# Which engine adds up the weights for a Strassen-like product: trading VectorE adds against DMA sums between two matrix products

## The chip, the cores and the metric

The kernel runs on one core of a Trainium2 chip. The metric is the device time of one execution in microseconds; lower is better. TensorE (PE) does the matrix products, VectorE (DVE) and ScalarE (ACT) prepare operands and empty PSUM, GpSimd (POOL) and SyncE (SP) mostly issue DMAs.

## The reference, cut to what matters

The reference is one layer of a streaming encoder on a (512, 1024) float32 stream: attention in two branches, a gated merge, then an MLP and a gated embedding, each with its RMSNorm. The change touches only the weights of the MLP:

```python
u = rms_norm(h, g_mlp)
h = h + jnp.square(jax.nn.relu(u @ w_ff1)) @ w_ff2      # w_ff1 (1024, 4096), w_ff2 (4096, 1024)
```

All of it is float32, and the tolerance asks for more than one rounded product, so every matrix is split into a rounded part (hi) and a remainder (lo), and each product is made as hi*hi + hi*lo + lo*hi.

## The kernel before, in words

**Seven products instead of eight.** ff1 (u @ w_ff1) and ff2 (... @ w_ff2) are cut into eight groups each of 512 hidden columns. A group's weights are a 2x2 arrangement of quadrants of [128, 1024] float32 (512 KB), named (0,0), (1,0), (0,1), (1,1). A group is made with seven products of sums, Winograd's form of Strassen's scheme, rather than eight plain ones. Products 1, 2 and 3 use a quadrant as it was loaded. The other four use sums that are made in place:

- product 5: (0,0) += (0,1)
- product 6: the same place += (1,1), after product 5's weights have been split
- product 4: the same place += (1,0), after product 6's weights have been split
- product 7: (0,1) += (1,1), after product 5's sum has read (0,1)

**Who makes a sum.** `sum_source` (line 276) makes it, either as `tensor_tensor` on VectorE (line 296) or as an accumulating DMA that GpSimd issues (line 298). Before the change: ff2's (key "s2") products 5 and 7 on VectorE, and ff1's group 1 products 6 and 7 too; all others by DMA. That is 18 VectorE sums and 46 DMAs in the feed-forward part. Eight further DMA sums are for the gates (`wgw`), earlier in the kernel.

**A split** (`emit_split`, lines 301 to 326) makes hi with a ScalarE cast (line 324) and lo with a VectorE subtraction (line 325). The traces name them `u<n>h` and `u<n>l`, n counting all weight units.

**Order.** The feed-forward part runs in four passes (fq = 0..3) of 28 products each. Pass fq has ff1's groups 2fq (letter a) and 2fq + 1 (letter b), and ff2's same groups (A and B):

```python
STEPS = "a1 b1 a2 a5 b5 b2 a6 b6 a7 a3 b7 b3 A1 a4 b4 B1 A2 A5 B5 B2 A6 B6 A3 A7 B7 B3 A4 B4"
```

Unit 53 is a1 of pass 0, and each pass has 28 units: u109 to u136 are pass 2. In it u113 is b5, u116 b6, u117 a7, u126 A5, u127 B5, u130 B6, u131 A3 and u132 A7. A product is 24 matmuls of 256 columns (`win_mm`, line 918, traced as `('f1', g)x`, y or z by its PSUM bank) or 12 of 512 (`s2_mm`, line 1331, `s_0x` and so on). Products 1, 6, 7 and 4 of a group add into the same bank x, and what they held is copied or drained in between: ff1 by `win_out` (lines 929 and 933), ff2 by `h_add` into the residual stream (lines 1073 and 1075) after the odd group.

**What sets the order.** Instructions of TensorE and GpSimd run in the order in which the program traces them. For VectorE, ScalarE and the loads on SP a planner puts them in order at build time by costs and due times of its own, in nearly all of the passes. On the chip every engine runs its list strictly in that order. In step n the main loop (line 1369) first takes out the product before, then splits the weights of step n + 2 (`advance`), offers step n + 3 to `sum_source` (line 388), and then traces product n.

`advance` also offers sums as soon as they may be made: after product 1's split product 5's sum, after 5's split those of 6 and 7, after 6's split that of 4. The condition in line 339 left ff2's 5 and 7 out of this; they came by line 388 (and the planner could still put them earlier on VectorE).

**Places.** Twelve places of 512 KB hold the quadrants; a load may start once the last reader of the quadrant before it has been split.

Of the kernel before, what the change touches and what calls it, by code (L numbers as in the profile page):

```python
# [50 lines left out]
def layer_kernel(ctx: ExitStack, tc: tile.TileContext, x, p, g_mix, w_in, b_forget, swa_sinks,  # L51
# [32 lines left out]
    raws, order, unit_of = [], [], {}  # L84
# [94 lines left out]
    def raws_of(i):  # L179
        r, pn = order[i][1][:2]  # L180
        if isinstance(r, dict):
            return [r[z] for z in {1: ((0, 0),), 2: ((1, 0),), 3: ((1, 1),),
                                   5: ((0, 0), (0, 1)), 6: ((0, 0), (1, 1)),
                                   7: ((0, 1), (1, 1)), 4: ((0, 0), (1, 0))}[pn]]
        if isinstance(r, list):
            return {1: r[:1], 2: r[1:], 3: r[1:]}.get(pn, r)
        return [r]
# [58 lines left out]
    def emit_dma(i):  # L246

        upto = max(first_raw[r] for r in raws_of(i))
        while look["d"] <= upto:
            r_ = used[look["d"]]  # L250
            r = raws[r_]
            if r_ in before and before[r_] >= look["n"]:
                return
            if first_ff <= r_ < last_ff:
                if "place" not in look:
                    return
                r["tile"] = ff_place(place_of[r_], r["shape"])
            elif place_of[r_]:
                if look["wp2"] is None:
                    return  # L260
                r["tile"] = look["wp2"].tile(r["shape"], F32, tag="w2_raw", bufs=2, name=r["name"])
            else:
                r["tile"] = wp.tile(r["shape"], F32, tag="w_raw", bufs=2, name=r["name"])
            for ks, src in r["fns"]:
                nc.sync.dma_start(r["tile"][:, ks], src)
            look["d"] += 1

    def quadrant(i, h, e):


        rs = order[i][1][0]
        return raws[rs[h]]["tile"][:, e] if isinstance(rs, list) else raws[rs[h, e]]["tile"]
# [3 lines left out]
    def sum_source(i):  # L276

        if i in sources or i >= len(order) or not isinstance(order[i][1][0], (list, dict)):  # L280
            return
        emit_dma(i)
        key, (rs, pn, _), _ = order[i]

        first = {5: 1, 6: 5, 4: 6}.get(pn)
        if (first and unit_of[key[:-1] + (first,)] >= look["n"]
                or pn == 7 and unit_of[key[:-1] + (5,)] not in sources
                or any(raws[r]["tile"] is None for r in raws_of(i))):
            return
        if pn in (1, 2, 3):  # L290
            q = quadrant(i, pn in (2, 3), pn == 3)
        else:
            q = quadrant(i, 0, pn == 7)
            other = quadrant(i, *{5: (0, 1), 7: (1, 1), 6: (1, 1), 4: (1, 0)}[pn])
            if key[0] == "s2" and pn in (5, 7) or key in (("f1", 1, 6), ("f1", 1, 7)):
                nc.vector.tensor_tensor(q, q, other, ALU.add)
            else:
                nc.gpsimd.dma_start(q, other, accum_op=ALU.add)  # L298
        sources[i] = q if key[0] == "s2" else q.rearrange("q k (j c) -> q k j c", c=P)

    def emit_split(i):
        _, (r, sl, shape), _ = order[i]
        emit_dma(i)
        if order[i][0] in early:
            hi, lo = early[order[i][0]]
        else:
            hi = wp.tile(shape, F32R, tag="w_hi", bufs=4, name=f"u{i}h")
            lo = wp.tile(shape, F32R, tag="w_lo", bufs=4, name=f"u{i}l")
        sum_source(i)
        src = sources[i] if isinstance(r, (list, dict)) else raws[r]["tile"][sl]  # L310
        if order[i][0][0] == "pg":

            for a in range(2):
                g = g_ple_t[:, 2 * order[i][0][2] + a:2 * order[i][0][2] + a + 1]
                nc.scalar.mul(hi[:, a], src[:, a], g)
                nc.vector.scalar_tensor_tensor(lo[:, a], src[:, a], g, hi[:, a].bitcast(F32),
                                               ALU.mult, ALU.subtract)
            order[i][2] = (hi, lo)
            return
        np_ = N_PIECES if i < 20 else 1  # L320
        for a in range(np_):
            n = shape[1] // np_
            z = slice(a * n, a * n + n)
            nc.scalar.copy(hi[:, z], src[:, z])
            nc.vector.tensor_tensor(lo[:, z], src[:, z], hi[:, z].bitcast(F32), ALU.subtract)  # L325
        order[i][2] = (hi, lo)

    def advance(i):

        while look["n"] < min(len(order), i + 1):  # L330
            n = look["n"]
            emit_split(n)
            look["n"] += 1
            emit_dma(min(len(order) - 1, look["n"] + look["ahead"]))
            if isinstance(order[n][1][0], (list, dict)):

                key = order[n][0]
                for pn in {1: (5,), 5: (6, 7), 6: (4,)}.get(key[-1], ()):
                    if key[0] != "s2" or pn in (6, 4):
                        sum_source(unit_of[key[:-1] + (pn,)])  # L340

    def unit(key):
        i = unit_of[key]
        advance(i + look["split"])
        if i == 0:
            emit_dma(look["dma"])
        return order[i][2]
# [674 lines left out]
    for t in P2_STEPS:  # L1022
        if t[0] == "ops":
            gate_ops(t[1])
            continue
        if t[0] == "fill":
            look["split"] = 2
            fill(t[1])
            look["split"] = 0
            continue  # L1030
        i = unit_of[t]
        if done is not None and done[0] == "g":
            gate_out(win_out(done[:3], done[3], tmp2), done[1])
        advance(i + 3)
        for n in range(look["n"], i + 9):
            sum_source(n)
        if t[0] == "br":
            branches(t[1])
            if t[1] == 5:
                h_sb = hp.tile([P, NT, D], F32, tag="h", bufs=1, name="h_sb")  # L1040
                nc.sync.dma_start(h_sb, x.rearrange("(t q) d -> q t d", q=P))
                gb = hp.tile([P, D], F32, tag="gb", bufs=1, name="g_mlp_bc")
                bcast_row(gb, g_mlp[0])
        else:
            win_mm(t[:3], t[3], [[o] for o in g_op[t[3]]], {})
        done = t
# [191 lines left out]
    for tb in range(NT - 1):  # L1238
        h2(tb, 1, row_group("psm", "mix", mix_t, 1, tb))
        scale2(tb)  # L1240
        if tb == 0:
            advance(unit_of["pp", 1])
        if tb > 0:
            t2_pe(tb - 1)
            t2_top(tb - 1)
# [272 lines left out]
```

## Time and profile before

| | |
|---|---|
| median of 3 runs | 715.89 us (715.85 to 716.19) |
| the profiled execution | 717.25 us, its span 715.3 us |
| busy: PE, DVE, ACT, POOL | 704.4, 532.7, 450.2, 84.8 us |
| granted TensorE clock, mean | 0.997 |
| the four passes | about 352 to 660 us |
| VectorE sums / DMA sums, feed-forward part | 18 / 46 |

The span is the time from the first instruction to the last; an execution takes some 2 us more. Rows of the timelines give the start in us, the duration, engine, line, operation, and in square brackets the idle time of the engine before it and what ended it. Rows of the chain of waits give start, length and what ran. "PEld" is the loading of weights into TensorE, which shows a wait for an operand first. The ends of matmuls are modelled, so a product's length is best taken from start to start.

### The profile page before, as it was taken

To read this page: it belongs to the slowest core of one execution; us is meant where nothing else is said; L and a number is where in the kernel's file an instruction comes from. 1 tells how busy PE (TensorE), PEld (TensorE's weight loads), DVE (VectorE), ACT (ScalarE), POOL (GpSimd) and SP (SyncE) were. 2 spreads that over 40 slices of the span, in tenths; PEclk is the share of its full clock that TensorE was granted. 3 is DMA by queue.
4 is the path that set the end of the run, shared out by engine and by line. 5 is a ranking of instruction groups with operands and counts; after the bars stand their busy time and mean duration, and the time that the engine had idled before them with its cause. 6 is when DMAs were issued, how large, how long until landed. Compare 5 with 4: busy or idle time off the path is not lost.

```text
span 715.3 us, 11466 instructions
## 1 busy us (share of the span) xinstructions
PE 704.4 (98%) x4229; PEld 626.4 (88%) x4229; DVE 532.7 (74%) x908; ACT 450.2 (63%) x839; POOL 84.8 (12%) x124
## 2 busy tenths in 40 slices
PE   8999999999999999999999999999999999999995
PEld 7988888888888998888899889988999789988885
DVE  6557888877696556545789985899579966997565
ACT  6547888779863554344788736874477546875452
POOL 1011211100001200001510102010300021010101
PEclk9999999999999999999999999999999999999998
DMA  9256456670364795450885598739894699079002
GB/s 288 70 164 159 115 125 158 151 196 1 119 206 118 147 320 181 152 172 31 238 188 193 111 288 160 239 86 256 185 253 119 152 243 233 34 148 351 3 22 96
DMA packets 74055, 115.67 MB, mean 162 GB/s; under 512 B 6664, under 2 KB 44560, under 8 KB 74000
## 3 DMA queue, kind: packets, MB, share of 16 engines
q1 hardware_dynamic: 65936, 86.24, 38.0%
q0 software_dynamic: 7776, 28.32, 21.5%
q8 instruction: 33, 0.54, 0.3%
q10 hardware_dynamic: 288, 0.39, 0.2%
q14 instruction: 22, 0.18, 0.1%
HBM read 72.93 MB, written 4.19 MB: 108 GB/s over the span
## 4 chain that ended last, share of the span: by engine, by line
PE 86%; DVE 6%; DMA 4%; issue 2%; ACT 1%; POOL 0%; SPq 0%; POOLq 0%; DVEq 0%; ACTq 0%
PE pf L74 5%; PE pf L76 5%; PE pf L75 5%; PE s_6x L1331 3%; PE s_0x L1331 3%; PE h_sc L760 3%; PE s_2x L1331 2%; PE h_pv L830 2%; PE h_tr L818 2%; PE psm L76 2%; PE psm L74 2%; PE psy L74 2%; PE psy L75 2%; PE psm L75 2%; PE psy L76 2%
## 5 line engine op out<-in xcount | busy, mean ns | idle before, releaser
L298 POOL DMA_DIRECT2D wq<-wq x24 | 21.8, 936 | 166.8 <-DVE u70l L325 25.9
L778 ACT ACTIVATE s<-s,h_nm 128x128 f32<-128x128 f32 (+1 forms) x64 | 32.6, 512 | 5.9 <-DVE h_nm L771 5.1
L71 DVE TENSOR_TENSOR h_ptl<-h_tr,h_pth 128x512 fp32r<-128x512 f32 (+2 forms) x40 | 22.9, 604 | 4.0 <-ACT h_pth L70 3.6
L359 POOL TENSOR_SCALAR n_ms<-acc 128x1 f32<-128x1 f32 x15 | 5.6, 373 | 163.8 <-ACT junk L1083 105.4
L70 ACT CAST h_pth<-h_tr 128x512 fp32r<-128x512 f32 (+2 forms) x40 | 19.4, 523 | 1.8 <-PE h_tr L818 1.4
L70 ACT CAST u<-n_tr 128x512 fp32r<-128x512 f32 (+2 forms) x26 | 12.6, 519 | 11.8 <-PE n_tr L1139 5.6
L474 PE MATMUL va<-wv_h,u 128*128 128x320 f32 x64 | 20.0, 317 | 0.0
L818 PE MATMUL h_tr<-ident,s 128*128 128x128 f32 x136 | 19.6, 277 | 0.2
L474 PE MATMUL vb<-wv_h,u 128*128 128x328 f32 x64 | 19.6, 313 | 0.0
L71 DVE TENSOR_TENSOR u<-n_tr,u 128x512 fp32r<-128x512 f32 (+2 forms) x26 | 15.0, 603 | 5.8 <-ACT u L70 5.7
L298 POOL DMA_DIRECT2D wgw<-wgw x8 | 7.1, 971 | 102.3 <-DVE u25l L325 77.7
L1083 ACT ACTIVATE junk<-h_sb 128x512 f32<-128x512 f32 x16 | 10.1, 630 | 12.6 <-DVE h_sb L1073 10.1
L830 PE MATMUL h_pv<-h_pth,v 128*128 128x256 f32 (+1 forms) x64 | 17.3, 291 | 0.0
L830 PE MATMUL h_pv<-h_ptl,v 128*128 128x256 f32 (+1 forms) x64 | 16.9, 305 | 0.3 <-DVE h_ptl L71 0.3
L818 PEld LDWEIGHTS h_tr<-ident,s 128*128 128x128 f32 x136 | 15.1, 141 | 2.0 <-ACT s L798 0.5
L1420 DVE TENSOR_TENSOR sgp<-sgp,pp 128x512 f32<-128x512 f32 (+1 forms) x9 | 5.7, 632 | 14.2 <-ACT sgp L1419 14.2
L1073 DVE TENSOR_TENSOR h_sb<-psm,h_sb 128x512 f32<-128x512 f32 x8 | 5.5, 689 | 13.8 <-PE psm L76 13.8
L798 ACT ACTIVATE s<-s,h_rec 128x128 f32<-128x128 f32 (+2 forms) x32 | 14.2, 483 | 2.4 <-DVE h_rec L792 2.4
L840 DVE TENSOR_TENSOR h_ao<-h_pv,h_ao 64x512 f32<-64x512 f32 x16 | 10.9, 681 | 6.0 <-ACT h_ao L839 5.8
L766 DVE CUSTOM_DVE_ANT_0 s<-h_sc,causal 128x128 f32<-128x128 f32 (+3 forms) x32 | 13.8, 483 | 0.3 <-PE h_sc L760 0.3
L792 DVE RECIPROCAL h_rec<-h_den 128x4 f32<-128x4 f32 x16 | 3.0, 185 | 14.5 <-ACT s L778 14.3
L830 PEld LDWEIGHTS h_pv<-h_ptl,v 128*128 128x128 f32 x64 | 12.1, 188 | 1.7 <-DVE h_ptl L71 0.8
(1609 smaller groups left out, 2774.9 us busy)
## 6 DMA issues: line engine op xcount, KB each, us to landing
wq<-in_w_ff_dram SPq DMA_DIRECT2D x45, 512.0 KB, 5.9
wq<-wq POOLq DMA_DIRECT2D x24, 512.0 KB, 5.9
wq_c<-in_w_ff_dram SPq DMA_DIRECT2D x9, 512.0 KB, 6.7
wg<-in_w_in_dram SPq DMA_DIRECT2D x4, 1024.0 KB, 5.3
wgw<-in_w_in_dram SPq DMA_DIRECT2D x8, 512.0 KB, 4.7
wgw<-wgw POOLq DMA_DIRECT2D x8, 512.0 KB, 5.8
wmix<-in_w_mix_out_dram SPq DMA_DIRECT2D x4, 1024.0 KB, 5.1
wpg<-in_w_ple_gate_dram SPq DMA_DIRECT2D x4, 1024.0 KB, 8.6
```

What stands on the lines that cost most here:

```text
L70: nc.scalar.copy(hi, src)
L71: nc.vector.tensor_tensor(lo, src, hi.bitcast(F32), ALU.subtract)
L74: nc.tensor.matmul(ps, lh, rh, start=start, stop=False)
L75: nc.tensor.matmul(ps, lh, rl, start=False, stop=False)
L76: nc.tensor.matmul(ps, ll, rh, start=False, stop=stop)
L298: nc.gpsimd.dma_start(q, other, accum_op=ALU.add)
L474: nc.tensor.matmul(ps, u[:, kk_, ts_], w[:, kk_, c0:c1], start=kk_ == 0 and n == 0, stop=kk_ == KT - 1 and n == 2)
L760: nc.tensor.matmul(ps[:, off:off + n], qs[i][z][:, qb * P:(qb + 1) * P], kk[i][z][:, k0:k0 + n], start=z == 0, stop=z == 1)
L778: nc.scalar.activation(sl, sl, AF.Exp, bias=nm[:, qb:qb + 1], accum_out=den[:, qb:qb + 1])
L818: nc.tensor.transpose(tr[:, n, :], c["s"][:, o, :], ident)
L830: nc.tensor.matmul(pv[:, q0:q0 + nq, :], V2[kb][:, c["v"], :], t[:, o:o + nq, :], start=n == 0, stop=n == 2 * NT - 1, skip_group_check=True)
L1331: nc.tensor.matmul(bank[g // 2, "2" + bk, i], o, w, start=tg != "" and n == 0, stop=n == 5, skip_group_check=True)
```

## The change

ff1's products 6 and 7 of all groups but group 0 go from DMAs to VectorE (group 1 had them there). ff2's products 5 and 7 go from VectorE to DMAs, and these are traced where `advance` first offers them: product 5's behind product 1's split, product 7's behind product 5's split, right after product 6's. After it there are 14 VectorE sums and 50 DMAs.

```diff
@@ sum_source
-            if key[0] == "s2" and pn in (5, 7) or key in (("f1", 1, 6), ("f1", 1, 7)):
+            if key[0] == "f1" and key[1] > 0 and pn in (6, 7):
                 nc.vector.tensor_tensor(q, q, other, ALU.add)
             else:
                 nc.gpsimd.dma_start(q, other, accum_op=ALU.add)
@@ advance
                 for pn in {1: (5,), 5: (6, 7), 6: (4,)}.get(key[-1], ()):
-                    if key[0] != "s2" or pn in (6, 4):
-                        sum_source(unit_of[key[:-1] + (pn,)])
+                    sum_source(unit_of[key[:-1] + (pn,)])
```

## The prediction

> **What bounds the kernel now.** I read the page's busy shares first, then the chain of waits from 330 to 660 us (the feed-forward passes), then each engine in order of time where that chain leaves TensorE.
>
> ```profile
> span 715.3 us, 11466 instructions
> PE 704.4 (98%) x4229; PEld 626.4 (88%) x4229; DVE 532.7 (74%) x908; ACT 450.2 (63%) x839; POOL 84.8 (12%) x124
> ...
> 352.31 2.77 PE ('f1', 0)x L918 x24
> 357.83 2.72 PE ('f1', 0)y L918 x24
> 406.91 5.47 PE s_0x L1331 x24
> 423.26 5.44 PE s_0x L1331 x24
> 428.70 2.77 PE ('f1', 2)x L918 x24
> 450.55 2.87 PE ('f1', 2)x L918 x24
> 461.90 2.72 PE s_2x L1331 x12
> 502.86 6.26 DMA wq<-wq
> 511.82 7.97 DMA wq<-wq
> 583.11 2.77 PE ('f1', 6)x L918 x24
> 656.80 0.87 PE n_tr L378 x8
> ```
>
> TensorE is busy 98% of the span, and a product takes 2.72 to 2.77 us whoever makes its weights. So the change can only take away, or add, time in which TensorE waits inside the four passes of 28 products. Pass 0 lasts 428.70 - 352.31 = 76.39 us. The fourth has no excess over it: 656.80 - 583.11 = 73.69 us to its last product, against 423.26 + 2.72 - 352.31 = 73.67 us. The second and third together take 583.11 - 428.70 = 154.41 us, which is 1.63 us more than twice 76.39. Of that, four products from 450.55 to 461.90 take 11.35 us where 4 x 2.72 is 10.88: 0.47 us of matmuls stretched evenly, with no wait that the trace shows. What is left, 1.16 us, is nearly all in the three gaps of the weight loads in the third pass (0.38 + 0.24 + 0.58 = 1.20):
>
> ```profile
> 527.69 0.30 PEld L918 LDWEIGHTS ('f1', 4)x<-at_ff,u117h 128*128 128x128 f32 x2 [0.38 <-ACT u_('f1', 4)_5727 L929]
> 555.12 0.19 PEld L1331 LDWEIGHTS s_4z<-u127h,o 128*128 128x128 f32 x1 [0.24 <-ACT o L70]
> 569.22 0.19 PEld L1331 LDWEIGHTS s_4x<-u132h,o 128*128 128x128 f32 x1 [0.58 <-issue]
> 519.87 1.05 ACT L324 CAST u116h<-wq 128x1024 fp32r<-128x1024 f32 x1 [2.94 <-DMA wq<-wq]
> 527.06 0.58 ACT L929 COPY u_('f1', 4)_5727<-('f1', 4)x 128x512 f32<-128x512 f32 x1
> 567.28 1.22 DVE L325 TENSOR_TENSOR u132l<-wq_c,u132h 128x1024 fp32r<-128x1024 f32 x1
> 568.42 1.28 DVE L1075 SCALAR_TENSOR_TENSOR h_sb<-s_4x,h_sb 128x512 f32<-128x512 f32 x2
> ```
>
> The first gap: ScalarE's cast for group 5's product 6 stood 2.94 us for a DMA sum, so ScalarE copied group 4's product 6 out of PSUM late (527.06), and product 7 adds into the same bank. The third: VectorE came to the drain of ff2's product 6 only at 568.42, and product 7 uses that bank. The second has the same root, VectorE's line of work in ff2:
>
> ```profile
> 352.10:384.90 32.80, 32.80 (x290) 32.76 (x290) 28.43 (x31) 26.82 (x39) 4.82 (x5) 1.00 0.88 239
> 505.50:538.70 33.20, 33.02 (x290) 32.82 (x288) 21.53 (x23) 22.27 (x30) 5.23 (x6) 1.00 0.88 208
> 538.70:583.00 44.30, 44.12 (x219) 36.94 (x218) 41.93 (x53) 26.68 (x34) 5.17 (x6) 1.00 0.68 178
> ```
>
> Columns: stretch, length, then busy time of PE, PEld, DVE, ACT, POOL, then clock, DMA share and GB/s. The first two are the stretches up to ff2's first product in passes 0 and 2, the third the ff2 part of pass 2. The granted clock is 1.00 throughout, so the clock is not the cause. In the ff2 part VectorE is busy 41.93 of 44.30 us (95%); before it, 21.53 of 33.20.
>
> **The change part by part.** Four VectorE sums a pass leave ff2; four (two for each group) come to ff1 in passes 1 to 3. Pass 0 has them for group 1 already, and group 0 keeps its DMAs.
>
> ```profile
> 352.10:428.50 76.40, 7.23 (x6) 1.00 0.77 205
> 428.50:505.50 77.00, 4.89 (x4) 1.00 0.76 191
> q0 software_dynamic: 7776, 28.32, 21.5%
> L298 POOL DMA_DIRECT2D wq<-wq x24: 852/862/1212, 347.3 to 635.2; - x24
> 509.32 0.86 POOL L298 DMA_DIRECT2D wq<-wq  x1 [5.60 <-DVE u112l L325]
> 511.82 1.75 POOL L298 DMA_DIRECT2D wq<-wq  x2 [0.75 <-DVE u113l L325]
> 548.64 0.86 POOL L298 DMA_DIRECT2D wq<-wq  x1 [25.30 <-DVE u126l L325]
> 551.10 0.86 POOL L298 DMA_DIRECT2D wq<-wq  x1 [1.60 <-DVE u127l L325]
> 537.24 1.23 DVE L296 TENSOR_TENSOR wq_c<-wq_c,wq 128x1024 f32<-128x1024 f32 x1 [0.71 <-DMA wq<-in_w_ff_dram]
> ```
>
> 1. VectorE sums (the first two rows, line 296 alone): 4.89 / 4 = 1.22 us each. ff2 loses 4 x 1.22 = 4.89 us of VectorE a pass: 41.93 becomes 37.04 of 44.30 us, 84%. It also loses the place where VectorE stood 0.71 us for a load. The late bank drain and the late operand then come up to 4.9 us earlier: second and third gap gone.
> 2. ff1 of passes 1 to 3 gains 4.89 us of VectorE: 21.53 becomes 26.42 of 33.20, 80%. Pass 0 already ran at 28.43 of 32.80 with products of 2.72 us, so the cover is there. Price: nothing on TensorE. A sum for product 7 reads what product 5's DMA sum leaves alone but must let it finish reading; should VectorE wait for that, it waits no longer than the cast of product 5's weights, which it needs next anyway.
> 3. ff1 loses 4 DMA sums a pass in passes 1 to 3, 12 in all. The casts of products 6 then wait for a 1.22 us add and not for the third DMA of a burst: the 2.94 us stand of ScalarE goes, and with it the first gap. What is late next there is product 5's own sum, still a DMA (6.26 us in the chain of waits), which no product waited for.
> 4. ff2 gains 16 DMA sums, four a pass, and the queue has 4 more than before. Each takes GpSimd about 0.86 us (1.21 behind another). GpSimd is 12% busy; nothing else stands in its queue in these passes before the norms behind the last one. In the DMA engines a sum costs 21.5% of 715.3 us / 54 sums (46 here, 8 of the gates) = 2.85 us, so the ff2 part's share goes from 0.68 to about 0.68 + 4 x 2.85 / 44.30 = 0.94, and ff1's falls from 0.88 to 0.54. SP's loads for the next pass share this; they are wanted a whole part later.
> 5. Product 5's sums in ff2 are issued alone, right behind product 1's split, three to five products ahead of use. Row for a sum by itself: 548.64 to its cast at 553.24 (below), 4.6 us. Three products are 8.2 us. Nothing on TensorE.
> 6. Products 6 and 7 in ff2 are now issued as four in a row (A6, A7, B6, B7) where two stood apart. That is the unknown cost, and it falls on B6, third in the line. The nearest rows are the same burst in ff1:
>
> ```profile
> 510.31 1.23 DVE L325 TENSOR_TENSOR u113l<-wq,u113h 128x1024 fp32r<-128x1024 f32 x1 [1.27 <-ACT u113h L324]
> 520.96 1.22 DVE L325 TENSOR_TENSOR u116l<-wq,u116h 128x1024 fp32r<-128x1024 f32 x1 [3.30 <-ACT u116h L324]
> 394.96 1.22 DVE L325 TENSOR_TENSOR u71l<-wq_c,u71h 128x1024 fp32r<-128x1024 f32 x1
> 553.24 1.05 ACT L324 CAST u129h<-wq 128x1024 fp32r<-128x1024 f32 x1 [0.57 <-DMA wq<-wq]
> 556.01 1.05 ACT L324 CAST u130h<-wq 128x1024 fp32r<-128x1024 f32 x1 [0.94 <-DMA wq<-wq]
> DMA to landing us min/median/max: 4.5/5.8/11.0
> ```
>
> There product 6 of the second group was split 522.18 - 511.54 = 10.64 us after the split of product 5. In ff2 of pass 0, B5's split ends at 396.18 and B6 starts at 406.91 + 5.47 / 2 = 409.65: 13.47 us to spend. It holds by 2.8 us. ScalarE stands some 3 us at B6 (its cast could run at 511.54 + 8.33, that is 8.3 us behind B5's split, against 556.01 - 550.81 = 5.2 now), with the casts of the operands for B6, A7 and A3 behind it; they fit in the same 2.8 us, since VectorE no longer makes them late. Bounds: nothing (the burst as in ff1), or, with the longest landing of 11.0 us where the burst's was 7.97, 3.0 us later: 3.0 - 2.8 = 0.2 us a pass, 0.8 us in all. I take nothing, since the burst is the nearer row and ff2 has the emptier DMA engines.
>
> The row for GpSimd's issue at 548.64 shows 0.86 us while VectorE worked without a break, as does the one at 509.32, where VectorE had pauses. [...]
>
> The sum: -1.16 us, +0. The profiled execution took 717.25 us, 1.95 more than its span; it would take 716.09. The median of the runs is 715.89, so 714.7.
>
> **The rivals.**
> - Nothing moves (715.9): the gaps belong to the third pass alone, and the first and fourth show none with the same code. Runs without the profiler may have none either: 715.89 less the 1.95 outside the span is 713.94, below 715.3. Against it: the late cast and the late drain are there in the order of work.
> - All excess goes, the stretched products too: 1.63 us, 714.3. For it: they stand at the end of ff1, beside loads. Against: pass 0 has loads there at an equal DMA share, and no stretch.
> - Slower: ScalarE's stand for B6's sum takes TensorE with it. It decides once B6's split comes over 13.47 us behind B5's, that is when the sum lands 2.8 us later than in ff1's burst (7.97 + 2.8 = 10.8 us, just under the longest row). ff2's fuller engines (0.94) speak for it, beyond my bound of 0.8 us: at 12 us it would cost 1.2 us a pass, 4.9 in all, less 1.16: 719.6; at 11.5 us 0.7 a pass, 2.8 in all: 717.5, which I take for this case. Three products of lead in ff1 against the same three here speak against it.
> - Starved issue: each issue held up by one of VectorE's instructions, 1.22 us. B6's, the third, would come 3.66 us late, 0.86 over the room, 3.4 us in all: 718.1. The row at 548.64 speaks against.
>
> **How the numbers follow.** A measurement here can tell about 0.2%, 1.43 us, from no change: faster is below 714.46, slower above 717.32. Chances: forecast 0.42, nothing moves 0.24, all excess gone 0.17, slower by B6 0.14, starved issue 0.03. Faster: 0.17 and a small end of the forecast, 0.04: 0.21. Slower 0.17, less the 0.01 in which B6 costs too little to count: 0.16. Same: the rest, 0.63. The range goes from 714.1, just under the case with all excess gone, to 717.5, the middle of the slower case, leaving out its upper half and the last rival. The forecast's own range is 714.3 to 715.5, with the 0.8 us bound on top.
>
> **What would show it.** VectorE near 37 us in the ff2 part of the third pass and 26 before it; the three gaps of the weight loads gone, and passes of 76.4 us each; 50 DMA sums and 14 VectorE sums; casts of ff1's products 6 no longer waiting for DMAs; B6's cast waiting about 3 us for its sum, with no gap on TensorE behind it. I am wrong if TensorE shows gaps at ff2's products 5, 6 or 3 that a DMA sum or a cast behind one released, or if VectorE's new sums stand on a DMA for longer than a product.

## The result and the profile after

| | before | after |
|---|---|---|
| median | 715.87 us (715.42 to 716.19, 4 runs) | 720.53 us (719.69 to 721.29, 4 runs) |
| ratio | | 1.0065, interval 1.0052 to 1.0078 |
| profiled execution, its span | 717.25, 715.3 us | 720.79, 719.0 us |

The change makes the kernel slower by 4.7 us, where 1.2 us less was forecast. The profiled execution of before was 1.4 us over its own median, so a comparison of the two profiles shows only 3.7 us of it. The page of the changed kernel, its span, busy shares and GpSimd's DMA queue:

```profile
span 719.0 us, 11452 instructions
PE 705.2 (98%) x4229; PEld 626.6 (87%) x4229; DVE 529.9 (74%) x904; ACT 448.3 (62%) x839; POOL 87.5 (12%) x128
q0 software_dynamic: 8352, 30.41, 22.9%
```

VectorE has four instructions fewer and GpSimd four more, as counted: 14 VectorE sums and 50 DMA sums. The next view cuts the changed kernel into stretches: up to ff2's first product and from there on, for passes 1, 2 and 3 (columns as in the prediction):

```profile
428.45:462.62 34.17, 33.42 (x290) 33.23 (x288) 27.05 (x28) 23.37 (x33) 2.58 (x3) 1.00 0.63 165
462.62:506.94 44.32, 44.09 (x219) 36.91 (x217) 36.67 (x47) 25.32 (x32) 7.80 (x9) 1.00 0.82 200
506.94:541.22 34.28, 33.43 (x290) 33.23 (x288) 27.05 (x28) 23.36 (x33) 2.58 (x3) 1.00 0.67 173
541.22:584.93 43.71, 43.71 (x218) 36.99 (x217) 36.68 (x47) 25.27 (x32) 7.80 (x9) 1.00 0.86 208
584.93:618.19 33.26, 33.26 (x289) 33.22 (x288) 27.05 (x28) 23.57 (x33) 2.58 (x3) 1.00 0.54 128
618.19:660.38 42.19, 42.02 (x215) 35.49 (x213) 34.94 (x46) 26.61 (x42) 6.53 (x9) 1.00 0.80 204
```

The yardstick is a pass without any stall, as the first experiment below has them: 32.73 us, then 43.67 us (41.75 up to the last product of the fourth pass). Against it ff1 loses 1.44, 1.55 and 0.53 us (3.52 together), and ff2 0.65, 0.04 and 0.44, with 0.08 more in pass 0 (1.2 together). The profile of the kernel before was 1.6 us above the same yardstick. Behind the passes the last store lands 0.3 us later than in that experiment, counted from the last product's start (56.2 against 55.9 us). The other 0.9 us between the two spans lies behind that landing, where no work is left: 2.4 us here, 1.6 there. The granted clock is 1.00 in all six stretches.

So most of the loss is in ff1, where the forecast had put nothing. The timeline of VectorE, ScalarE and the weight loads in pass 1 (u83 is product 2 of the even group, u89 its product 7), then VectorE's sum in pass 3 and the weight load for product 7 in pass 2:

```profile
430.42 1.23 DVE L296 TENSOR_TENSOR wq<-wq,wq 128x1024 f32<-128x1024 f32 x1 [4.91 <-DMA wq<-wq]
432.16 1.22 DVE L325 TENSOR_TENSOR u83l<-wq,u83h 128x1024 fp32r<-128x1024 f32 x1
441.55 0.63 ACT L1283 ACTIVATE u_('f1', 2)_4768<-u_('f1', 2)_4768 128x512 f32<-128x512 f32 x1 [3.00 <-DVE u_('f1', 2)_4768 L932]
450.58 0.58 ACT L928 COPY u_('f1', 2)_4970<-('f1', 2)x 128x512 f32<-128x512 f32 x1
451.21 0.30 PEld L917 LDWEIGHTS ('f1', 2)x<-at_ff,u89h 128*128 128x128 f32 x2 [0.94 <-ACT u_('f1', 2)_4970 L928]
585.99 1.23 DVE L296 TENSOR_TENSOR wq_c<-wq_c,wq_gb 128x1024 f32<-128x1024 f32 x1 [3.99 <-DMA wq<-wq_c]
529.81 0.30 PEld L917 LDWEIGHTS ('f1', 4)x<-at_ff,u117h 128*128 128x128 f32 x2 [1.05 <-ACT u_('f1', 4)_5727 L928]
```

The planner has put the new sum for product 7 (line 296) ahead of product 2's split in VectorE's list. The sum overwrites what product 5's DMA sum reads, so VectorE stands 4.91 us for that DMA, with all its other work behind it. It does not catch up before the end of ff1. ScalarE stands 3.00 us for a product taken out late, copies product 6 out of its bank late (450.58), and TensorE stands 0.94 us. The products behind the stall then take 2.83 to 2.93 instead of 2.72 us from start to start until ff1 ends, which is the rest of the 1.44. Pass 2 goes the same way. In pass 3 VectorE stands 3.99 us and the trace shows no wait of TensorE in ff1; the 0.53 us lost there are slower products alone.

In ff2 the late work is the one the prediction had named (u102 is B6, u103 A3, u104 A7):

```profile
481.37 1.05 ACT L324 CAST u102h<-wq_c 128x1024 fp32r<-128x1024 f32 x1 [3.28 <-DMA wq_c<-wq]
482.97 0.69 DVE L71 TENSOR_TENSOR o<-u_('f1', 3)_4802,o 128x512 fp32r<-128x512 f32 x1 [1.58 <-ACT o L70]
490.18 0.19 PEld L1330 LDWEIGHTS s_2z<-u103l,o 128*128 128x128 f32 x1 [0.27 <-DVE u103l L325]
492.39 1.28 DVE L1074 SCALAR_TENSOR_TENSOR h_sb<-s_2x,h_sb 128x512 f32<-128x512 f32 x2
493.19 0.19 PEld L1330 LDWEIGHTS s_2x<-u104h,o 128*128 128x128 f32 x1 [0.63 <-issue]
648.58 0.19 PEld L1330 LDWEIGHTS s_6x<-u160h,o 128*128 128x128 f32 x1 [0.57 <-issue]
664.30 0.42 PEld L377 LDWEIGHTS n_tr<-ident,h_sb 128*128 128x128 f32 x4 [0.74 <-DVE u L71]
```

ScalarE stands 3.28 us for B6's sum, third in the line of four. The operand casts behind it come late, VectorE stands 1.58 us for one of them, and product 3's lo weights and the drain of product 6's bank (492.39, two halves) end just after TensorE wants them. The wait before product 7 (493.19) has no releaser in the trace; that it is for this drain is read from the bank, s_2x, which product 7 writes next. The last row lies behind the four passes: the transposes of the next norm wait 0.74 us for VectorE, where it was 0.20 in the kernel before.

### The profile page after: what moved, and what is told of

It is laid out like the page before. It is cut to its first block, busy times and chain, and to the rows that moved or that the text cites. A ratio compares the mean times of both kernels' runs of the same rounds, so it can differ in the third digit from the quotient of the medians.

```text
span 719.0 us, 11452 instructions
## 1 busy us (share of the span) xinstructions
PE 705.2 (98%) x4229; PEld 626.6 (87%) x4229; DVE 529.9 (74%) x904; ACT 448.3 (62%) x839; POOL 87.5 (12%) x128
## 4 chain that ended last, share of the span: by engine, by line
PE 72%; issue 8%; DVE 8%; DMA 7%; ACT 3%; POOL 0%; SPq 0%; POOLq 0%; ACTq 0%; DVEq 0%
PE pf L74 5%; PE pf L76 5%; PE pf L75 5%; PE s_4x L1330 3%; PE h_sc L759 2%; PE h_pv L829 2%; PE h_tr L817 2%; PE psm L74 2%; PE psm L75 2%; PE psm L76 2%; PE psy L74 2%; PE psy L75 2%; PE psy L76 2%; DMA wq<-wq 2%; DMA wq_c<-wq 2%
## 5 line engine op out<-in xcount | busy, mean ns | idle before, releaser
L298 POOL DMA_DIRECT2D wq<-wq x21 | 19.2, 928 | 100.5 <-DVE u87l L325 16.3
L296 DVE TENSOR_TENSOR wq<-wq,wq 128x1024 f32<-128x1024 f32 x9 | 10.7, 1219 | 4.9 <-DMA wq<-wq 4.9
L791 DVE RECIPROCAL h_rec<-h_den 128x4 f32<-128x4 f32 x16 | 3.0, 184 | 14.5 <-ACT s L777 14.3
```

## The experiments

The theory after this reading: the burst A6, A7, B6, B7 makes B6 late and costs ff2; product 7's sum, put ahead of product 2's split, costs ff1. The rivals: ff1's part is harmless by itself and something of ff2's makes it cost; or the burst is harmless, and one queue or engine is simply too full.

**1. ff1's part alone.** ff1's sums as in the change, ff2's as before.

```diff
-            if key[0] == "f1" and key[1] > 0 and pn in (6, 7):
+            if key[0] == "s2" and pn in (5, 7) or key[0] == "f1" and key[1] > 0 and pn in (6, 7):
...
-                    sum_source(unit_of[key[:-1] + (pn,)])
+                    if key[0] != "s2" or pn in (6, 4):
+                        sum_source(unit_of[key[:-1] + (pn,)])
```

> ff1's products 6 and 7 summed on VectorE for groups 1 to 7, ff2's sums as before. Theory A (VectorE stands in ff1 for product 5's DMA sum, because product 7's sum was put ahead of product 2's split, as seen for 4.91 us in the changed kernel): the stand stays, and with it the excess of the ff1 parts, 3.5 us over three passes: 718.5 to 719.5. Rival B (the burst of four DMA sums in ff2 is what costs): none of it here, so 715.0 to 716.2.

Measured: 714.70 us (714.33 to 715.57, 11 runs) against 715.62 for before, ratio 0.9986 (0.9978 to 0.9995). It is faster than before, by 0.92 us, and below both expected ranges. Its ff1 part of pass 1, and VectorE's sums for product 7 in passes 1 and 2:

```profile
428.25:460.98 32.73, 32.73 (x289) 32.72 (x288) 27.83 (x29) 22.76 (x31) 1.72 (x2) 1.00 0.53 144
428.03 1.23 DVE L297 TENSOR_TENSOR wq<-wq,wq 128x1024 f32<-128x1024 f32 x1 [2.71 <-DMA wq<-wq]
505.24 1.23 DVE L297 TENSOR_TENSOR wq_gb<-wq_gb,wq 128x1024 f32<-128x1024 f32 x1 [3.52 <-DMA wq<-wq_gb]
```

My expectation was wrong. VectorE's list puts the sum in the same place and VectorE stands there too, 2.71 and 3.52 us, yet no product of any pass is late. So the place in the list is not enough to cost time; whether ff2's part makes the stand longer is tested below.

**2. ff2's part alone.** ff2's sums as in the change, ff1's as before (condition `key in (("f1", 1, 6), ("f1", 1, 7))`).

> ff2's products 5 and 7 by early DMAs, ff1 as before (group 1 on VectorE). Theory A: ff2's part of the loss is 1.2 us in the passes and up to 0.7 us behind them, so 716.5 to 717.5. Rival B: all of the loss, 719.5 to 720.5.

Measured: 718.54 us (717.77 to 719.97, 5 runs), ratio 1.0046 (1.0033 to 1.0058), 2.9 us slower.

```profile
461.14:505.47 44.33, 44.11 (x218) 36.91 (x217) 38.46 (x49) 25.52 (x33) 7.79 (x9) 1.00 0.85 212
505.47:539.73 34.26, 33.02 (x289) 32.82 (x288) 21.11 (x23) 23.04 (x32) 6.07 (x7) 1.00 0.94 219
479.93 1.05 ACT L324 CAST u102h<-wq_c 128x1024 fp32r<-128x1024 f32 x1 [3.30 <-DMA wq_c<-wq]
528.73 0.30 PEld L917 LDWEIGHTS ('f1', 4)x<-at_ff,u117h 128*128 128x128 f32 x2 [1.44 <-ACT u_('f1', 4)_5727 L928]
```

B6's stand and ff2's 44.3 us are those of the full change: that part of the loss comes from ff2's edit alone. The time lies between the two expected ranges, since ff1 loses 1.5 us in pass 2 here too, though ff1's sums are made as before. There ScalarE's casts wait for DMA sums (product 6's for 2.33 us), and its copy of product 6 out of the bank is late, as in the first gap of the kernel before. So ff2's edit reaches ff1 also without VectorE's new sum.

**3. Product 7's sum held back in ff1.** The changed kernel, with the sum issued only behind product 5's split.

```diff
-                nc.vector.tensor_tensor(q, q, other, ALU.add)
+                with tc.issue_after(lo_ins[unit_of[key[:-1] + (5,)]].ins) if pn == 7 else ExitStack():
+                    nc.vector.tensor_tensor(q, q, other, ALU.add)
```

> The changed kernel, but in ff1 product 7's VectorE sum is queued behind product 5's split (issue order alone). Theory A: VectorE no longer stands ahead of product 2's split, the ff1 excess goes, and 1.2 to 1.9 us of ff2 and tail are left: 717.0 to 718.0. Rival C (ff1's loss is VectorE's extra work, 4.9 us a pass, wherever it stands): no change from 720.5.

Measured: 718.30 us (717.84 to 718.61, 5 runs), ratio 1.0038 (1.0025 to 1.0050), 2.2 us less than the changed kernel. The ff1 part of pass 1:

```profile
428.54:461.27 32.73, 32.73 (x290) 32.73 (x288) 25.39 (x27) 23.15 (x32) 2.58 (x3) 1.00 0.66 171
```

ff1's loss goes (32.73; 0.3 us is left in pass 2), ff2's stays (44.34 us in pass 1): in the changed kernel VectorE's stand is what carries the loss into ff1. The time is 0.3 us above the range expected.

**4. ff2's product 7 offered late.** The changed kernel, with `advance` not offering ff2's product 7, so that its sums come from line 388.

```diff
-                    sum_source(unit_of[key[:-1] + (pn,)])
+                    if key[0] != "s2" or pn != 7:
+                        sum_source(unit_of[key[:-1] + (pn,)])
```

> The changed kernel, but ff2's product 7 DMA sums are offered late (by the main loop), so that product 6's sums are no longer followed and preceded by them in GpSimd's queue. Theory A with the burst as the ff2 part: B6's cast stands about 0.9 us and not 3, the gaps at ff2's products 3 and 7 shrink, 719.0 to 719.8. If the burst costs nothing: 720.5.

Measured: 738.75 us, ratio 1.0325 (1.0311 to 1.0339). A miss: in GpSimd's list these sums now stand behind product 4's sums, and TensorE waits over 4 us for the weights in every pass:

```profile
418.33 0.19 PEld L1331 LDWEIGHTS s_0x<-u76h,o 128*128 128x128 f32 x1 [3.46 <-ACT u76h L324]
```

It says nothing on the burst, only that a DMA sum must not be traced behind one that waits for later work.

**5. The same four sums in another order.** ff2's part alone, but issued as A6, B6, A7, B7: the sums of both groups' product 7 are offered after B5's split.

```diff
-                    sum_source(unit_of[key[:-1] + (pn,)])
+                    if key[0] == "f1" or pn != 7:
+                        sum_source(unit_of[key[:-1] + (pn,)])
+                    elif key[1] % 2:
+                        for g in (key[1] - 1, key[1]):
+                            sum_source(unit_of["s2", g, 7])
```

> ff2's products 5 and 7 by early DMAs, ff1 as before, but ff2's sums are issued in the order A6, B6, A7, B7, so that B6's is second in GpSimd's queue and not third. Theory A (what ff2 pays is ScalarE standing some 3 us at B6's cast for the third of four queued DMA sums, the operands' casts behind it, and VectorE with them): the stand shrinks to 1 to 2 us, the gaps at ff2's products 3 and 7 go; 716.0 to 717.2. Rival D (four more sums a pass load the DMA engines, in whatever order): 718.5, as in the ff2 part alone.

Measured: 716.52 us (716.15 to 717.01, 11 runs), ratio 1.0008 (0.9999 to 1.0017): no difference from before that can be told, and about 2 us less than experiment 2.

```profile
477.63 1.06 ACT L324 CAST u102h<-wq_c 128x1024 fp32r<-128x1024 f32 x1 [1.19 <-PE s_2z L1334]
```

B6's cast no longer waits for a DMA, and all four passes have the lengths of the yardstick, 2.9 us less than in experiment 2. The number of sums is the same; B6's place in the line was the cost. That the time is 1.8 us above experiment 1's with passes of the same lengths comes from behind the passes: 59.3 us from the last product's start to the end of the span, against 57.4, with the norm's transposes waiting 1.80 us for VectorE against 0.40.

**6 and 7. One half of ff2's part each, with ff1's part.** In 6 product 5 goes to early DMAs and product 7 stays on VectorE; in 7 product 7 goes and product 5 stays (`key[0] == "s2" and pn == 7`, then `pn == 5`, stays on VectorE and is not offered by `advance`).

> ff1's part, and of ff2's part product 5 alone by early DMAs; ff2's product 7 stays on VectorE. Theory A: no burst of four, B6's cast stands as before (about 1 us), so nothing is lost against ff1's part alone: 714.5 to 715.2. Rival D: half of ff2's loss, 715.8 to 716.5.

> ff1's part, and of ff2's part product 7 alone by early DMAs (the burst A6, A7, B6, B7); ff2's product 5 stays on VectorE. Theory A: the burst brings all of ff2's loss, 716.5 to 718.0. Rival D: half of it, 715.8 to 716.5.

Measured: 736.35 us, ratio 1.0290 (1.0276 to 1.0304), for 6; 719.47 us (718.56 to 720.04, 5 runs), ratio 1.0048 (1.0035 to 1.0062), for 7. First 6, in ff2 of pass 0:

```profile
386.23 1.23 DVE L297 TENSOR_TENSOR wq_gb<-wq_gb,wq 128x1024 f32<-128x1024 f32 x1 [3.90 <-DMA wq<-wq_gb]
396.38 1.23 DVE L297 TENSOR_TENSOR wq<-wq,wq 128x1024 f32<-128x1024 f32 x1 [1.54 <-DMA wq_c<-wq]
405.52 0.19 PEld L1332 LDWEIGHTS s_0z<-u71h,o 128*128 128x128 f32 x1 [2.85 <-ACT o L70]
```

Miss for 6: product 7's VectorE sums follow DMAs of product 5 again, here in ff2, and VectorE stands 3.90 and 1.54 us for them; operands then come 1.55 and 2.85 us late. So 6 says nothing on the burst. In 7 the burst is whole, and most of the loss is there, 3.6 us against before; that is above the range expected, which had counted ff2's part alone. VectorE's stand in ff1 of pass 1:

```profile
430.40 1.23 DVE L297 TENSOR_TENSOR wq<-wq,wq 128x1024 f32<-128x1024 f32 x1 [4.78 <-DMA wq<-wq]
```

Product 7's DMAs alone bring the late B6 (its cast stood 3.02 us in that pass) and the long stand in ff1. Product 5's early sums aren't needed for either.

**8. A first try to make the stand longer.** Experiment 1 with a 512 KB copy to HBM traced ahead of each sum for ff1's product 5.

> ff1's part alone, with an extra 512 KB copy to HBM queued by GpSimd ahead of each of ff1's product 5 sums in passes 1 to 3; the copy's result is not used. It makes those sums land about 1.9 us later and touches nothing in ff2. Theory E (the changed kernel loses in ff1 because product 5's sum lands 2.2 us later there than in ff1's part alone, and VectorE stands for it ahead of other work, 4.9 us and not 2.7): VectorE stands 4 to 5 us in each of three passes, and the excess in ff1 is 0.5 to 1.5 us a pass: 716.2 to 718. Rival (the loss in ff1 needs something else of the ff2 part): 714.5 to 715.0.

Measured: 714.84 us (714.29 to 715.33, 11 runs), ratio 0.9983 (0.9975 to 0.9992). Inconclusive: the copies waited only for a load and went out early, so VectorE stood 0.44 us longer than in experiment 1 in pass 1 and no longer in passes 2 and 3.

```profile
428.47 1.23 DVE L298 TENSOR_TENSOR wq<-wq,wq 128x1024 f32<-128x1024 f32 x1 [3.15 <-DMA wq<-wq]
```

**9. The changed kernel with two issues swapped.** Experiment 5's order of the burst in the full change. In the feed-forward part the lists of TensorE, VectorE, ScalarE and SP are the changed kernel's, one for one; only GpSimd's differs.

> The changed kernel with one thing altered: ff2's sums behind the splits of product 5 are issued as A6, B6, A7, B7 instead of A6, A7, B6, B7. VectorE's and ScalarE's lists are those of the changed kernel, with product 7's sum in ff1 still ahead of product 2's split. Theory: B6's late sum is the one root of both losses. B6 lands in about 5 us, ScalarE stands for it no longer than in the kernel before, ff2 takes 43.7 us in each pass; the loads for the next pass start on time, product 5's sum in ff1 lands within 0.6 us of a1's start, VectorE stands at most 3.2 us for it and ff1 takes 32.73 us. Passes 76.4, 76.4, 76.4, 74.5; with a tail of 58.7 to 59.3 us the time is 715.5 to 716.5. Rival 1: VectorE's order in ff1 costs by itself: ff1 stays at 33.3 to 34.3 us in passes 1 to 3 and the time is 718 to 719.5. Rival 2: the four sums cost ff2 in any order: ff2 stays at 44.3 and the time is 718.5 or more.

Measured: 717.34 us (716.96 to 717.67, 10 runs), ratio 1.0019 (1.0009 to 1.0028): 3.2 us less than the changed kernel. The two parts of pass 1, B6's cast in pass 0, the stand in ff1, and the norm behind the passes:

```profile
429.09:461.82 32.73, 32.73 (x289) 32.72 (x288) 26.32 (x28) 23.30 (x32) 2.58 (x3) 1.00 0.63 163
461.82:505.49 43.67, 43.67 (x218) 37.08 (x217) 37.72 (x48) 25.75 (x33) 7.79 (x9) 1.00 0.89 216
402.07 1.06 ACT L324 CAST u74h<-wq_c 128x1024 fp32r<-128x1024 f32 x1 [1.15 <-PE s_0z L1334]
428.40 1.23 DVE L296 TENSOR_TENSOR wq<-wq,wq 128x1024 f32<-128x1024 f32 x1 [2.24 <-DMA wq<-wq]
661.18 0.42 PEld L381 LDWEIGHTS n_tr<-ident,h_sb 128*128 128x128 f32 x4 [1.62 <-DVE u L71]
```

Every pass is clean, ff1 too, though nothing in ff1 was touched: the passes together take 4.7 us less than in the changed kernel, of which 0.9 us are lost again behind them and 0.7 us ahead of them. So both losses have one root, B6's late sum. How it reaches the next pass can be followed in the rows between. First the changed kernel: B6's cast (u74) in pass 0, the next sum in line (it waits for u74's lo), what SP's load queue waited for in 409 to 423 us, the first load that follows, and the load queue's share of the DMA engines while product 5's sum is under way (423.14 to 430.40):

```profile
402.89 1.05 ACT L324 CAST u74h<-wq_c 128x1024 fp32r<-128x1024 f32 x1 [2.70 <-DMA wq_c<-wq]
408.65 0.86 POOL L298 DMA_DIRECT2D wq_c<-wq  x1 [4.36 <-DVE u74l L325]
SPq L265 <- DMA wq_c<-wq: 4.1, 1, 4.1
414.19 0.90 SPq L265 DMA_DIRECT2D wq<-in_w_ff_dram  x2
q1 hardware_dynamic: 701, 1.18, 43.0%
```

And in experiment 9, the same rows (product 5's sum under way from 423.78 to 428.38):

```profile
408.30 0.86 POOL L298 DMA_DIRECT2D wq_c<-wq  x1 [3.28 <-DVE u74l L325]
SPq L265 <- DMA wq_c<-wq: 2.1, 1, 2.1
413.21 0.90 SPq L265 DMA_DIRECT2D wq<-in_w_ff_dram  x2
q1 hardware_dynamic: 267, 0.50, 29.6%
```

B6's split late makes product 4's sum late (GpSimd); that sum frees places, and SP's loads for the next pass wait for it; from the next pass's first product backwards they start 14.3 us ahead instead of 15.9 (428.45 - 414.19, 429.09 - 413.21). So 1.18 MB of loads (all within the first 4.6 us) instead of 0.50 run beside product 5's sum in ff1, which takes 7.3 us instead of 4.6, and VectorE stands 4.91 us instead of 2.24. No run changed the loads alone, so this link is read from the rows. Passes 1 to 3 of the other profiles agree with it: where the loads start 15.8 to 15.9 us ahead (experiments 5 and 9) the sum takes 4.6 to 5.6 us, at 14.8 to 15.0 (before and experiment 1) 5.1 to 6.6, and at 13.1 to 14.3 (the changed kernel and experiment 2) 6.4 to 8.1.

The time was 0.8 us above the range expected. The passes took what was forecast. The profile starts them 0.7 us later than in the changed kernel, with nothing altered ahead of them, and has 59.5 us behind the last product's start where 58.7 to 59.3 were expected; why the start is later stays open. Behind the passes the norm's transposes wait 1.62 us for VectorE, against 0.40 in experiment 1. Their cast stands behind one more split in ScalarE's list than there (as in the changed kernel), with ScalarE held up by the load of those split weights. A version with experiment 1's order at that place wasn't tried.

**10. Product 5's sum issued later.** Experiment 1, with a 128 KB copy that waits for product 1's split traced ahead of product 5's sum of the even groups.

```diff
+                if key[0] == "f1" and key[1] in (2, 4, 6) and pn == 5:
+                    lo1 = order[unit_of[key[:-1] + (1,)]][2][1]
+                    nc.gpsimd.dma_start(late_out[key[1] // 2 - 1], lo1[:, 0, :2].bitcast(F32))
                 nc.gpsimd.dma_start(q, other, accum_op=ALU.add)
```

> ff1's part of the change alone (ff2 as before), and in passes 1 to 3 GpSimd first copies 128 KB of a1's lo weights to HBM, behind a1's split and ahead of product 5's sum of the same group: that sum is issued about 1 us later and lands 1.2 to 1.7 us later. VectorE's list is that of ff1's part alone. Theory: the length of VectorE's stand for that sum decides. Without the copy it stands 2.71 us in pass 1 and costs nothing; with it 3.9 to 4.5 us, near the 4.91 us of the changed kernel, and the ff1 part of passes 1 to 3 grows by 0.1 to 1.0 us each: 715.2 to 717. Rival: VectorE catches up whatever the stand, the loss in the changed kernel's ff1 came by another way (its ff2 backlog): ff1 stays at 32.73 us, 714.4 to 715.0.

Measured: 715.03 us (714.42 to 717.48, 12 runs), ratio 0.9995 (0.9985 to 1.0004). As a whole undecided: most runs are near experiment 1's time, two lie over 2 us above it. The profiled execution is one of those two (717.48), and its passes differ among themselves, so they can be compared with each other. The ff1 parts of passes 1 to 3, VectorE's three stands, and the weight loads for product 7 in passes 2 and 3:

```profile
428.74:461.48 32.74, 32.74 (x290) 32.73 (x289) 27.87 (x29) 22.90 (x31) 1.70 (x2) 1.00 0.55 148
505.14:539.22 34.08, 33.01 (x289) 32.81 (x288) 27.86 (x29) 22.57 (x31) 1.71 (x2) 1.00 0.53 143
582.89:616.57 33.68, 33.02 (x290) 32.81 (x288) 27.86 (x29) 22.57 (x31) 1.71 (x2) 1.00 0.43 108
429.16 1.23 DVE L298 TENSOR_TENSOR wq<-wq,wq 128x1024 f32<-128x1024 f32 x1 [3.35 <-DMA wq<-wq]
507.43 1.23 DVE L298 TENSOR_TENSOR wq_gb<-wq_gb,wq 128x1024 f32<-128x1024 f32 x1 [5.21 <-DMA wq<-wq_gb]
584.77 1.23 DVE L298 TENSOR_TENSOR wq_c<-wq_c,wq_gb 128x1024 f32<-128x1024 f32 x1 [4.81 <-DMA wq<-wq_c]
528.22 0.30 PEld L923 LDWEIGHTS ('f1', 4)x<-at_ff,u117h 128*128 128x128 f32 x2 [1.26 <-ACT u_('f1', 4)_5729 L934]
605.57 0.30 PEld L923 LDWEIGHTS ('f1', 6)x<-at_ff,u145h 128*128 128x128 f32 x2 [0.86 <-ACT u_('f1', 6)_6487 L934]
```

A stand of 3.35 us costs nothing; 5.21 and 4.81 us cost 1.35 and 0.95, by the same wait for the copy of product 6. The copy delays the sum's issue by 0.6 us in each pass; what made the stands of passes 2 and 3 longer by 1.4 to 1.7 us than experiment 1's is not shown. With the other kernels: in experiments 1, 8 and 9 stands up to 3.52 us are free; 4.03 us (experiment 7, pass 3) cost 0.18 and the changed kernel's 3.99 us in pass 3 0.53, both without a wait that the trace shows; 4.78 and 5.59 us (experiment 7) cost 0.89 and 1.74, and the changed kernel's 4.91 and 5.01 us 1.44 and 1.55. The cost goes with the length of the stand, and it begins between 3.5 and 4.0 us.

## Why the prediction was wrong

The step that failed is step 6: B6's third place in the burst, taken as nothing with a bound of 0.8 us. It measured about 2 us in ff2's part alone (experiment 2 less experiment 5) and 3.2 us in the full change (the changed kernel less experiment 9); in the passes of the profiles alone it is 2.9 and 4.7 us, more than half of it in ff1.

- **The forecast term of -1.16 us** came out about right in size, but not by the division that the steps gave. Where ff1's part is made alone, the three gaps go and so do the stretched products: 1.6 us in the passes of the profile, and 0.92 us (0.36 to 1.57) against the runs of before. Step 1 had put the second and third gap down to ff2's VectorE sums; they go in experiment 1, which keeps those sums. Step 3 had put the first gap down to ff1's DMA sums; it goes in experiment 5, which keeps those. Why either edit clears all of them stays open. That the size agrees is in part luck, since the 1.16 us came from one execution that was 1.4 us over its median.
- **Step 1** was right on VectorE's load: 36.68 us in the ff2 part of pass 2, 37.04 forecast. The bank drain did not become early, since the same edit made the operand casts ahead of it late. In experiment 9, with B6 on time, ff2 is clean.
- **Step 2** priced VectorE's new work in ff1 at nothing, which holds in experiments 1 and 9, and but for 0.3 us in 3. Its sentence on product 7's sum failed: it compared the stand with a cast that VectorE needs "next anyway". What stands next in VectorE's list is product 2's split, wanted six products ahead of product 7. I had not looked up where the planner would put the sum.
- **Step 3** was right that the casts of product 6 would be freed, and wrong that nobody waits for product 5's sum: VectorE does, and without that stand all but 0.3 us of the 3.5 us lost in ff1 is gone (experiment 3).
- **Step 4**: the DMA share in ff2 was 0.82 and 0.86 in passes 1 and 2, forecast 0.94; in ff1 it was 0.63 and 0.67, forecast 0.54. The sentence that SP's loads "are wanted a whole part later" was the second error. The loads aren't wanted early, but they start late and then share the engines with a sum that is wanted.
- **Step 5** held: experiments 5 and 9 keep these sums, and their passes are clean. What no step had is the order behind the passes: from the last product's start to the last store's landing the change cost 0.5 us as it stands, and 1.4 us in experiment 9, against 55.7 us before.
- **Step 6**: B6's 13.47 us of room was counted to B6's own product, and B6's cast did fit into it: no product 6 was late. The room of what stands behind that cast in ScalarE's list was not counted. Operand casts and product 3's split come through the same list, VectorE's work follows them, and so product 3's lo weights and the drain of product 6's bank were late first. The prediction said of the operands' casts "they fit in the same 2.8 us"; what stands behind them did not, by 0.3 and 0.6 us in pass 1.
- **The slower rival** (B6's cast, 717.5) had the right place with the wrong victim, and a price without the next pass. The range ended there.
- **Starved issue**: GpSimd's issues took 0.86 us in ff2 as before (408.65 above). The Trainium skill (SBUF — State Buffer, "SBUF: two separate sides") warns that a DMA issued from GpSimd gets no descriptors while VectorE runs an operation in a two-port performance mode. No run here shows such a starved issue; the late sums waited in line or for the DMA engines.

## What to carry to other kernels

A transfer moved into a line of transfers is priced by its place in that line, and its lateness by everything that stands behind the waiting instruction, through to the next pass's loads. When a sum moves to an engine with an in-order list, find out what it waits for and what it was put ahead of; engine time to spare is no answer to that. Swapping two issues brought back 3.2 of 4.7 us, and the best version (714.70 us) was half of the change.

## What the runs showed that I had not expected

- Four sums of 512 KB queued within 4 us land in order: in pass 1 of the changed kernel 4.6, 7.0, 7.3 and 9.2 us after their issue. In experiment 9 the second, B6, landed 5.0 us after its issue. For B6 the place in line was worth 2.3 us.
- In some passes the last products of ff1 take 2.83 instead of 2.72 us from start to start, at an unchanged granted clock of 1.00. In passes 1 and 2 of the changed kernel they follow a stall; in its pass 3, and in pass 1 of the kernel before, the trace shows no stall; and behind the stalls of experiments 2 and 10 only one product is slower. What causes it stays open.
- The order of work behind the passes cost about as much as the gaps that the change was to remove: experiments 5 and 9 have every pass at the yardstick and are still no faster than before.
